# Row-wise top-10 indices: input tiles at 512-byte boundaries, batch decode spread over tiles, short last batches

## The chip, the cores and the metric

The kernel runs on one core of a Trainium2 chip. The metric is the device time of one execution, in microseconds (us): the median of three runs. Everything below on time comes from those runs and from one profiled execution of the kernel before the change.

## The reference

For every row of an 8192 x 8192 float32 matrix the reference returns the column indices of the ten largest values, ordered from the largest value down.

```python
def reference(x, k):                       # x: 8192 x 8192 float32, k = 10
    indices = np.argpartition(x, -k, axis=1)[:, -k:]
    values = np.take_along_axis(x, indices, axis=1)
    sorted_idx = np.argsort(-values, axis=1)
    return np.take_along_axis(indices, sorted_idx, axis=1)
```

The input is 268.4 MB and each element is needed once; the output is 8192 x 10 int64, 0.66 MB.

## The kernel before

The 8192 rows are worked on in 64 tiles of 128 rows. A tile is loaded as 128 partitions x 8192 float32 in such a way that one row of x is spread over eight partitions: a row is cut into R = 8 pieces of W = 1024 elements, and partition p = 8a + q holds piece q of sixteen - divided into S = 8 slots - rows. So in each partition a tile has eight runs of 4096 bytes, one for each slot. `load` (L83) issues four transfers of two slots each on the SP queue (eight of one slot for the first and the last tile). Four buffers `xt` take the tiles in turn. `load(t + 3)` is issued in the loop at tile t, and SP waits there until the gather of tile t - 1 has read the buffer for the last time.

One pass over tile t goes through these functions:

- `weigh` (L133): ScalarE computes e = exp(36 x - 169.2) of half a tile at a time (bf16, two halves), and TensorE adds up, with the 0/1 matrix `group`, the weights of the eight pieces of each row: 16 matmuls of 512 columns give `s`, which has one row of x per partition and one column per position within a piece. The largest elements dominate these sums.
- `choose` (L152): VectorE finds the G = 12 best columns of `s` for each row (MAX8, MATCH_REPLACE8, FIND_INDEX8 on 1024 elements, twice); `cidb` keeps the columns of a batch of tiles, `idx` those of this tile.
- `gather` (L178): GpSimd fetches these columns of all eight pieces out of `xt` into `cand`. It is the last reader of the `xt` buffer.
- `spread` (L190): VectorE (six columns) and GpSimd (the other six) multiply `cand` by a mask; `extract` (L204): 12 TensorE products bring the 12 x 8 candidates of a row together in `g`.
- `rank` (L211): VectorE finds the ten best of the 96 candidates and their places `posb`. This is done three tiles late (LAG = 3), step by step between the steps of `choose`.

What remains is done for a batch of TB = 8 tiles at once. `decode` (L229) turns places into column numbers with seven VectorE instructions, ending with `rows`; `deliver` (L263) moves the results of each tile of the batch to the partition of their row with one matmul `fo` each (two on the engine, for the two passes of float32); `store` (L273) copies `fo` into `opack` and writes it to DRAM from the ScalarE queue. The batches are tiles 0 to 7, 8 to 15, ..., 56 to 62, and 63 alone.

The order on every engine is the order in which the loop (L291 to L324) is written; no scheduler moves anything inside it. In tile t the loop does: `choose(t)` with `rank(t - 3)` between its steps, `spread(t - 1)`, `gather(t)`, `weigh(t + 1)`, `store` of a batch delivered in an earlier tile, `extract(t - 1)`, `deliver` of a batch decoded in an earlier tile, `decode` of a batch whose last tile was just ranked, `load(t + 3)`. Behind the loop stand the last ranks, the batch of seven tiles, the spread and extract of tile 63, and its own batch of one. At the very end a count of checks (L328 to L345) decides whether an exact, slow path runs; it does not run here.

SBUF is handed out pool by pool: `consts`, `e`, `small`, `batch`, then `x`. In the built program the four `xt` buffers begin at byte 95904, 128672, 161440 and 194208 of each partition, which is 160 past a multiple of 512 each.

Of the kernel before, what the change touches and what calls it, by code (L numbers as in the profile page):

```python
# [10 lines left out]
P = 128  # L11
N = 8192
R = 8
A = P // R
S = P // A
W = N // R
BANK = 512
KMAX = 10
G = 12
TB = 8  # L20
# [3 lines left out]
FINITE = 1e37  # L24
BIG_NEG = -1e30
LAG = 3


@with_exitstack
def kernel(  # L30
# [29 lines left out]
    epool = ctx.enter_context(tc.tile_pool(name="e", bufs=3))  # L60
    small = ctx.enter_context(tc.tile_pool(name="small", bufs=2))
    bpool = ctx.enter_context(tc.tile_pool(name="batch", bufs=2))
    xpool = ctx.enter_context(tc.tile_pool(name="x", bufs=4))
    spsum = ctx.enter_context(
        tc.tile_pool(name="spsum", bufs=2, space=bass.MemoryType.PSUM)
# [7 lines left out]

    last = ntiles - 1

    starts = list(range(0, ntiles, TB)) + [last]
    sizes = [b - a for a, b in zip(starts, starts[1:] + [ntiles])]
    batch_of = {t: b for b, t0 in enumerate(starts) for t in range(t0, t0 + sizes[b])}

# [53 lines left out]
    def weigh(t):  # L133
        ss[t] = spsum.tile([P, W], fp32, tag="s", name="s")
        parts = [S // 4, S // 4, S // 4, S // 8, S // 8] if t == last else [S // 2, S // 2]
        s0 = 0
        for h, n in enumerate(parts):
            e = epool.tile([P, S // 2, W], bf16, tag="e", name="e")
            nc.scalar.activation(  # L139
                out=e[:, 0:n, :].rearrange("p s j -> p (s j)"),  # L140
                in_=xts[t][:, s0 * W:(s0 + n) * W],
                func=ACTF.Exp, bias=bias[:, 0:1], scale=BETA,
                accum_out=eall[:, 2 * t + h:2 * t + h + 1],
            )
            for i in range(n):
                for j in range(0, W, BANK):
                    nc.tensor.matmul(ss[t][:, j:j + BANK], lhsT=group[:, s0 + i, :],  # L147
                                     rhs=e[:, i, j:j + BANK],
                                     start=s0 + i == 0, stop=s0 + i == S - 1)
            s0 += n  # L150

    def choose_steps(t):  # L152
        m = ss.pop(t)
        b = batch_of[t]
        i = t - starts[b]
        if i == 0:
            batch[b] = (
                bpool.tile([P, TB, 16], u16, tag="cidb", name="cidb"),
                bpool.tile([P, TB, 16], u16, tag="posb", name="posb"),
            )  # L160
        cid = batch[b][0][:, i, :]
        w16 = wall[:, t, :]
        m2 = small.tile([P, W], fp32, tag="m2", name="m2")
        idxs[t] = small.tile([P, G], u16, tag="idx", name="idx")
        return [
            lambda: nc.vector.max(out=w16[:, 0:8], in_=m),  # L166
            lambda: nc.vector.match_replace(out=m2, in_to_replace=w16[:, 0:8], in_values=m,  # L167
                                            imm_value=-1.0),
            lambda: nc.vector.max_index(out=cid[:, 0:8], in_max=w16[:, 0:8], in_values=m),  # L169
            lambda: nc.vector.max(out=w16[:, 8:16], in_=m2),  # L170
            lambda: nc.vector.max_index(out=cid[:, 8:16], in_max=w16[:, 8:16], in_values=m2),  # L171
            lambda: nc.vector.tensor_scalar(
                out=idxs[t], in0=cid[:, 0:G], scalar1=float(W - 1), scalar2=base,
                op0=ALU.min, op1=ALU.add,
            ),
        ]
# [11 lines left out]
        del xts[t], idxs[t]  # L188

    def spread(t):  # L190
        shape = [P, G, P // 16, 16]
        masked[t] = small.tile(shape, fp32, tag="masked", name="masked")
        cand = cands.pop(t)
        half = G // 2
        shape = [P, half, P // 16, 16]
        for eng, g0 in ((nc.vector, 0), (nc.gpsimd, half)):
            eng.tensor_tensor(  # L197
                out=masked[t][:, g0:g0 + half],
                in0=cand[:, g0:g0 + half].unsqueeze(2).to_broadcast(shape),
                in1=own.rearrange("p (c s) -> p c s", s=16).unsqueeze(1).to_broadcast(shape),  # L200
                op=ALU.mult,
            )

    def extract(t):  # L204
        mk = masked.pop(t)
        gs[t] = gpsum.tile([P, G, R], fp32, tag="g", name="g")
        for c in range(G):
            nc.tensor.matmul(gs[t][:, c, :], lhsT=mk[:, c, :, :].rearrange("p a s -> p (a s)"),  # L208
                             rhs=place, start=True, stop=True)
# [16 lines left out]
                                          in_=t8b[:, KMAX - 9:KMAX - 8]),  # L226
        ]

    def decode(b):  # L229
        cidb, posb = batch.pop(b)  # L230
        n = sizes[b]
        slot = bpool.tile([P, TB, KMAX], u16, tag="slot", name="slot")[:, 0:n, :]
        low = bpool.tile([P, TB, KMAX], u16, tag="low", name="low")[:, 0:n, :]
        nc.vector.tensor_scalar(out=slot, in0=posb[:, 0:n, 0:KMAX],
                                scalar1=R.bit_length() - 1,
                                scalar2=None, op0=ALU.logical_shift_right)
        nc.vector.tensor_scalar(out=low, in0=posb[:, 0:n, 0:KMAX], scalar1=R - 1,
                                scalar2=None, op0=ALU.bitwise_and)
        shape = [P, n, KMAX, G]
        hot = bpool.tile([P, TB, KMAX, G], fp16, tag="hot", name="hot")[:, 0:n]  # L240
        pick = bpool.tile([P, TB, KMAX], fp32, tag="pick", name="pick")[:, 0:n, :]
        nc.vector.tensor_tensor(
            out=hot, in0=slot.unsqueeze(3).to_broadcast(shape),
            in1=slots.unsqueeze(1).unsqueeze(1).to_broadcast(shape), op=ALU.is_equal,
        )
        nc.vector.tensor_tensor(
            out=hot, in0=hot, in1=cidb[:, 0:n, 0:G].unsqueeze(2).to_broadcast(shape),
            op=ALU.mult,
        )
        nc.vector.reduce_sum(out=pick, in_=hot, axis=X_AX)  # L250
        val = bpool.tile([P, TB, KMAX], fp32, tag="val", name="val")[:, 0:n, :]
        nc.vector.scalar_tensor_tensor(
            out=val, in0=low, scalar=float(W), in1=pick, op0=ALU.mult, op1=ALU.add,
        )
        shape = [P, n, A, KMAX]
        picked[b] = bpool.tile([P, TB, A, KMAX], fp32, tag="rows", name="rows")
        nc.vector.tensor_tensor(  # L257
            out=picked[b][:, 0:n], in0=val.unsqueeze(2).to_broadcast(shape),
            in1=own_a.unsqueeze(1).unsqueeze(3).to_broadcast(shape), op=ALU.mult,
        )  # L260


    def deliver(b):  # L263
        n = sizes[b]
        rows = picked.pop(b)
        fo = fpsum.tile([P, A * KMAX], fp32, tag="fo", name="fo")[0:n * S, :]
        for i in range(n):
            nc.tensor.matmul(fo, lhsT=send[:, i, 0:n * S],  # L268
                             rhs=rows[:, i].rearrange("p a k -> p (a k)"),
                             start=i == 0, stop=i == n - 1)  # L270
        ready[b] = fo

    def store(b):  # L273
        n = sizes[b]
        o = opacks[b % 2][0:n * S]
        nc.vector.tensor_copy(out=o[:, :, :, 0],
                              in_=ready.pop(b).rearrange("p (a k) -> p a k", k=KMAX))
        r0 = starts[b] * S
        nc.scalar.dma_start(out=out_rows[r0:r0 + n * S, :],
                            in_=o.rearrange("p a k two -> p (a k two)"))  # L280

    def interleave(*lists):
        for group_ in zip(*[l for l in lists if l]):
# [3 lines left out]
    def run(steps):  # L287
        for step in steps:
            step()

    with tc.manual_schedule():  # L291
        weigh(0)
        for t in range(ntiles):
            second = rank_steps(t - LAG) if t >= LAG else []
            if t == last:
                run(second)
                second = []
            interleave(choose_steps(t), second)
            if t >= 1:
                spread(t - 1)  # L300
            gather(t)
            if t + 1 < ntiles:
                weigh(t + 1)
            for b in list(ready):
                store(b)
            if t >= 1:
                extract(t - 1)
            for b in list(picked):
                deliver(b)
            if t >= LAG and batch_of[t - LAG] != batch_of[t - LAG + 1]:  # L310
                decode(batch_of[t - LAG])
            if t + 3 < ntiles:
                load(t + 3)
        run(rank_steps(last - 2))
        run(rank_steps(last - 1))
        decode(batch_of[last - 1])
        deliver(batch_of[last - 1])
        store(batch_of[last - 1])
        spread(last)
        extract(last)  # L320
        run(rank_steps(last))
        decode(batch_of[last])
        deliver(batch_of[last])
        store(batch_of[last])  # L324

# [72 lines left out]
```

## Time and profile before

| | us |
|---|---|
| median of 3 runs (lowest, highest) | 713.9 (712.68, 715.07) |
| the profiled execution | 710.63 |
| its span, first to last instruction | 708.9 |

The profiled execution is 3.3 us under the median and 2.05 us under the lowest of the three runs; 1.7 us of it lie around the span.

| engine | busy us | share of the span |
|---|---|---|
| TensorE matmul | 558.8 | 79% |
| VectorE | 559.1 | 79% |
| ScalarE | 488.9 | 69% |
| GpSimd | 180.3 | 25% |
| DMA, queue of the x loads | | 95.1% of 16 engines |

Busy time is an average over the whole span. In the profile's rows PE is the matmul side of TensorE and PEld its weight loads, DVE is VectorE, ACT ScalarE, POOL GpSimd, SP the engine that issues the x loads; a q behind an engine's name is its sequencer or queue. A DMA share over 1 means that one packet's record overlaps the next one's.

### The profile page before, as it was taken

How to read it: one execution, taken by the hardware profiler on the slowest of the kernel's cores; microseconds unless marked ns; L12 is line 12 of the kernel's file. 1: busy time of each engine (PE TensorE's matmuls, PEld its weight loads, DVE VectorE, ACT ScalarE, POOL GpSimd, SP SyncE). 2: the span in 40 equal slices, each digit the busy share in tenths (PEclk: the TensorE clock that was granted, in tenths of full speed). 3: DMA queues.
4: the chain of work that ended last, by engine and by line, in shares of the span. 5: the costliest groups of instructions: out<-in, count | busy, mean ns of one | idle time of the engine just before them, and what ended most of it. 6: DMA issues, size and time to landing. Idle time of an engine off the chain costs nothing.

```text
span 708.9 us, 7965 instructions
## 1 busy us (share of the span) xinstructions
PE 558.8 (79%) x2690; PEld 348.3 (49%) x2690; DVE 559.1 (79%) x1313; ACT 488.9 (69%) x264; POOL 180.3 (25%) x135
## 2 busy tenths in 40 slices
PE   1678988697798978788888887869877887888844
PEld 0245665464454655455556644536543653555533
DVE  1568777987879878896788887798868976888973
ACT  4777776767777677776777777677777777776800
POOL 0121322321331332233132223213322322313330
PEclk9667777987666868887777877688888786667955
DMA  8999999999999999999999999999999999999400
GB/s 350 410 408 410 408 410 408 410 409 410 409 409 409 409 409 409 410 409 409 409 409 409 408 410 409 409 409 409 410 409 409 406 408 409 410 409 386 160 1 5
DMA packets 70592, 269.69 MB, mean 380 GB/s; under 512 B 4374, under 2 KB 5014, under 8 KB 70550
## 3 DMA queue, kind: packets, MB, share of 16 engines
q1 hardware_dynamic: 69760, 268.45, 95.1%
q10 hardware_dynamic: 790, 0.73, 0.4%
q8 instruction: 21, 0.34, 0.2%
q14 instruction: 21, 0.17, 0.1%
HBM read 268.51 MB, written 0.66 MB: 380 GB/s over the span
## 4 chain that ended last, share of the span: by engine, by line
DMA 52%; DVE 22%; PE 11%; SPq 5%; ACT 4%; issue 3%; POOL 2%; ACTq 0%
DMA xt<-in_x_dram 50%; PE s L147 6%; SPq L89 5%; ACT e L139 4%; PE g L208 4%; DVE wall L166 3%; DVE m L167 3%; DVE cidb L171 2%; DVE cidb L169 2%; DMA out_dram<-opack 2%; DVE wall L170 2%; POOL cand L180 2%; DVE masked L197 2%; DVE rows L257 1%; PE fo L268 1%
## 5 line engine op out<-in xcount | busy, mean ns | idle before, releaser
L139 ACT ACTIVATE e<-xt,bias 128x4096 bf16<-128x4096 f32 (+2 forms) x131 | 475.5, 3630 | 173.5 <-DMA xt<-in_x_dram 161.0
L147 PE MATMUL s<-e,group 128*128 128x512 bf16 x1024 | 340.3, 495 | 125.6 <-ACT e L139 125.4
L147 PEld LDWEIGHTS <-group 128*128 128x128 bf16 x1024 | 124.1, 124 | 314.3 <-issue 258.0
L208 PEld LDWEIGHTS g<-cpack,masked 128*128 128x128 f32 x1536 | 208.9, 216 | 29.1 <-issue 13.9
L208 PE MATMUL g<-cpack,masked 128*128 128x8 f32 x1536 | 201.9, 270 | 11.7 <-DVE masked L197 11.6
L180 POOL INDIRECT_COPY cand<-xt,idx 128x192 f32 x64 | 64.0, 1001 | 500.9 <-DMA xt<-in_x_dram 181.8
L166 DVE MAX8 wall<-s 128x8 f32<-128x1024 f32 x64 | 78.8, 1231 | 128.9 <-PE s L147 128.9
L197 POOL TENSOR_TENSOR masked<-cand,cpack 128x768 f32<-128x768 f32 x64 | 115.4, 1802 | 5.3
L169 DVE FIND_INDEX8 cidb<-wall,s 128x8 uint16<-128x1024 f32 x64 | 78.2, 1222 | 0.0
L171 DVE FIND_INDEX8 cidb<-wall,m 128x8 uint16<-128x1024 f32 x64 | 77.9, 1217 | 0.0
L167 DVE MATCH_REPLACE8 m<-wall,s 128x1024 f32<-128x1024 f32 x64 | 77.6, 1213 | 0.0
L170 DVE MAX8 wall<-m 128x8 f32<-128x1024 f32 x64 | 77.2, 1207 | 0.0
L197 DVE TENSOR_TENSOR masked<-cand,cpack 128x768 f32<-128x768 f32 x64 | 60.6, 947 | 0.0
L268 PE MATMUL fo<-rows,send 128*64 128x160 f32 (+2 forms) x128 | 31.9, 432 | 9.5 <-DVE rows L257 9.5
L268 PEld LDWEIGHTS fo<-rows,send 128*64 128x64 f32 (+2 forms) x128 | 25.0, 203 | 13.2 <-DVE rows L257 6.2
L139 ACT ACTIVATION_READ_ACCUMULATOR e<-xt,bias 128x1 f32 x131 | 24.4, 187 | 0.0
L329 ACT ACTIVATE e<-tall,bias 128x64 f32<-128x64 f32 x1 | 0.3, 348 | 32.2 <-DVE tall L225 32.2
L219 DVE MAX8 t8a<-g 128x8 f32<-128x96 f32 x64 | 15.8, 248 | 8.1 <-PE g L208 8.1
L222 DVE FIND_INDEX8 posb<-t8a,g 128x8 uint16<-128x96 f32 x64 | 16.3, 255 | 0.0
L224 DVE FIND_INDEX8 posb<-t8b,g 128x8 uint16<-128x96 f32 x64 | 16.1, 251 | 0.0
L220 DVE MATCH_REPLACE8 g<-t8a,g 128x96 f32<-128x96 f32 x64 | 15.8, 247 | 0.0
L223 DVE MAX8 t8b<-g 128x8 f32<-128x96 f32 x64 | 15.5, 242 | 0.0
(36 smaller groups left out, 102.7 us busy)
## 6 DMA issues: line engine op xcount, KB each, us to landing
xt<-in_x_dram SPq DMA_DIRECT2D x248, 1024.0 KB, 17.1
xt<-in_x_dram SPq DMA_DIRECT2D x16, 512.0 KB, 7.4
out_dram<-opack ACTq DMA_DIRECT2D x7, 80.0 KB, 5.4
out_dram<-opack ACTq DMA_DIRECT2D x1, 70.0 KB
cpack<-topk_cpack ACTq DMA_DIRECT2D x1, 68.5 KB
out_dram<-opack ACTq DMA_DIRECT2D x1, 10.0 KB
```

The costliest lines, as they stand in the source:

```text
L89: nc.sync.dma_start(out=dst[:, s:s + n, :], in_=src[:, s:s + n, :])
L139: nc.scalar.activation(out=e[:, 0:n, :].rearrange("p s j -> p (s j)"), in_=xts[t][:, s0 * W:(s0 + n) * W], func=ACTF.Exp, bias=bias[:, 0:1 ...
L147: nc.tensor.matmul(ss[t][:, j:j + BANK], lhsT=group[:, s0 + i, :], rhs=e[:, i, j:j + BANK], start=s0 + i == 0, stop=s0 + i == S - 1)
L166: lambda: nc.vector.max(out=w16[:, 0:8], in_=m),
L167: lambda: nc.vector.match_replace(out=m2, in_to_replace=w16[:, 0:8], in_values=m, imm_value=-1.0),
L169: lambda: nc.vector.max_index(out=cid[:, 0:8], in_max=w16[:, 0:8], in_values=m),
L170: lambda: nc.vector.max(out=w16[:, 8:16], in_=m2),
L171: lambda: nc.vector.max_index(out=cid[:, 8:16], in_max=w16[:, 8:16], in_values=m2),
L180: nc.gpsimd.add_instruction(mybir.InstIndirectCopy(name=nc.get_next_instruction_name(), ins=[nc.gpsimd.lower_ap(xts[t]), nc.gpsimd.lower_a ...
L197: eng.tensor_tensor(out=masked[t][:, g0:g0 + half], in0=cand[:, g0:g0 + half].unsqueeze(2).to_broadcast(shape), in1=own.rearrange("p (c s) ...
L208: nc.tensor.matmul(gs[t][:, c, :], lhsT=mk[:, c, :, :].rearrange("p a s -> p (a s)"), rhs=place, start=True, stop=True)
L268: nc.tensor.matmul(fo, lhsT=send[:, i, 0:n * S], rhs=rows[:, i].rearrange("p a k -> p (a k)"), start=i == 0, stop=i == n - 1)
```

## The change

Three things change.

1. A tile `pad` of 88 float32 and a pool `chosen` stand ahead of the pool `x`. `cidb` and `posb` move into `chosen`, which has three buffers instead of two. In the built program `xt` now begins at byte 96768, 129536, 162304 and 195072: multiples of 512. Sizes, steps and the order of the loads stay as they were.
2. `decode`, `deliver` and `store` become one list of steps, `finish_steps`: seven VectorE steps, one matmul step per tile of the batch, a copy and the store. After a batch's last rank the list is put aside, and each of the following tiles runs three steps of it, between `extract` and `load`. For a batch of eight that is 17 steps: six tiles.
3. The batches at the end are tiles 56 to 60 (five), 61 and 62 (two) and 63 (one), instead of seven and one. Behind the loop come: what is left of the batch of 48 to 55; ranks of tiles 61 and 62; spread and extract of tile 63; the batch of five; the batch of two; the rank of tile 63; its batch of one.

```diff
+PAD = 88
...
+    pad = ctx.enter_context(tc.tile_pool(name="pad", bufs=1)).tile([P, PAD], fp32, name="pad")
+    nc.vector.memset(pad[:, 0:1], 0.0)
+    cpool = ctx.enter_context(tc.tile_pool(name="chosen", bufs=3))
     xpool = ctx.enter_context(tc.tile_pool(name="x", bufs=4))
...
-    starts = list(range(0, ntiles, TB)) + [last]
+    starts = list(range(0, ntiles, TB)) + [last - 2, last]
...
-                bpool.tile([P, TB, 16], u16, tag="cidb", name="cidb"),
-                bpool.tile([P, TB, 16], u16, tag="posb", name="posb"),
+                cpool.tile([P, TB, 16], u16, tag="cidb", name="cidb"),
+                cpool.tile([P, TB, 16], u16, tag="posb", name="posb"),
...
+    def finish_steps(b):
...
+        def move(i):
             nc.tensor.matmul(fo, lhsT=send[:, i, 0:n * S],
                              rhs=rows[:, i].rearrange("p a k -> p (a k)"),
                              start=i == 0, stop=i == n - 1)
...
+        return [
+            lambda: nc.vector.tensor_scalar(
+                out=slot, in0=posb[:, 0:n, 0:KMAX], scalar1=R.bit_length() - 1,
+                scalar2=None, op0=ALU.logical_shift_right),
...
+            lambda: nc.vector.tensor_tensor(
+                out=rows, in0=val.unsqueeze(2).to_broadcast(rshape),
+                in1=own_a.unsqueeze(1).unsqueeze(3).to_broadcast(rshape), op=ALU.mult),
+        ] + [lambda i=i: move(i) for i in range(n)] + [
+            lambda: nc.vector.tensor_copy(
+                out=o[:, :, :, 0], in_=fo.rearrange("p (a k) -> p a k", k=KMAX)),
+            lambda: nc.scalar.dma_start(out=out_rows[r0:r0 + n * S, :],
+                                        in_=o.rearrange("p a k two -> p (a k two)")),
+        ]
...
         weigh(0)
+        later = []
         for t in range(ntiles):
-            second = rank_steps(t - LAG) if t >= LAG else []
-            if t == last:
-                run(second)
-                second = []
+            second = rank_steps(t - LAG) if t >= LAG and t != last else []
             interleave(choose_steps(t), second)
...
-            for b in list(ready):
-                store(b)
             if t >= 1:
                 extract(t - 1)
-            for b in list(picked):
-                deliver(b)
-            if t >= LAG and batch_of[t - LAG] != batch_of[t - LAG + 1]:
-                decode(batch_of[t - LAG])
+            if t == last - 1:
+                run(rank_steps(last - 3))
+            for step in later[:3]:
+                step()
+            later = later[3:]
+            done = t - LAG
+            if t < last and done >= 0 and batch_of[done] != batch_of[done + 1]:
+                later += finish_steps(batch_of[done])
             if t + 3 < ntiles:
                 load(t + 3)
+        run(later)
+        later = finish_steps(batch_of[last - 3])
         run(rank_steps(last - 2))
         run(rank_steps(last - 1))
-        decode(batch_of[last - 1])
-        deliver(batch_of[last - 1])
-        store(batch_of[last - 1])
         spread(last)
         extract(last)
+        run(later)
+        run(finish_steps(batch_of[last - 1]))
         run(rank_steps(last))
-        decode(batch_of[last])
-        deliver(batch_of[last])
-        store(batch_of[last])
+        run(finish_steps(batch_of[last]))
```

VectorE at tiles 58 and 59, where the batch of tiles 48 to 55 has just been ranked. Before, the first row is the last one of tile 58's `spread`, and the last row begins `choose(59)`:

```order
L197 TENSOR_TENSOR masked<-cand,cpack 128x768
L234 TENSOR_SCALAR slot<-posb 128x80
L237 TENSOR_SCALAR low<-posb 128x80
L242 TENSOR_TENSOR hot<-slot,slots 128x960
L246 TENSOR_TENSOR hot<-hot,cidb 128x960
L250 TENSOR_REDUCE pick<-hot 128x80
L252 SCALAR_TENSOR_TENSOR val<-low,pick 128x80
L257 TENSOR_TENSOR rows<-val,cpack 128x1280
L166 MAX wall<-s 128x8
```

With the change, from the end of tile 59 to the beginning of tile 60:

```order
L201 TENSOR_TENSOR masked<-cand,cpack 128x768
L255 TENSOR_SCALAR slot<-posb 128x80
L258 TENSOR_SCALAR low<-posb 128x80
L261 TENSOR_TENSOR hot<-slot,slots 128x960
L171 MAX wall<-s 128x8
```

The first three of the seven instructions stand one tile later than before; the next three follow at the end of tile 60, and `rows` at the end of tile 61.

VectorE behind `choose(63)`, the last one (`idx` is its last step, the `masked` row is `spread(62)`). Before:

```order
L172 TENSOR_SCALAR idx<-cidb,cpack 128x12
L197 TENSOR_TENSOR masked<-cand,cpack 128x768
L219 MAX t8a<-g 128x8
L220 MATCH_REPLACE g_4181<-t8a,g 128x96
L222 MAX_INDEX posb<-t8a,g 128x8
L223 MAX t8b<-g_4181 128x8
```

With the change:

```order
L177 TENSOR_SCALAR idx<-cidb,cpack 128x12
L201 TENSOR_TENSOR masked<-cand,cpack 128x768
L274 CAST opack_139<-fo 64x160
L223 MAX t8a<-g 128x8
L224 MATCH_REPLACE g_4198<-t8a,g 128x96
L226 MAX_INDEX posb<-t8a,g 128x8
```

The copy of the results of tiles 48 to 55 now stands ahead of `rank(61)`; before it stood at the end of tile 60.

TensorE at the end, before (L208 is `extract`, the first row those of tiles 62 - its first 12 are tile 61's - and L268 the matmuls `fo`):

```order
L208 MATMUL g<-cpack,masked 128x8 x24
L268 MATMUL fo<-rows,send 56x160 x7
L208 MATMUL g<-cpack,masked 128x8 x12
L268 MATMUL fo<-rows,send 8x160
L341 MATMUL gps<-ones,ngood_4268 1x1
```

With the change:

```order
L212 MATMUL g<-cpack,masked 128x8 x12
L250 MATMUL fo<-rows,send 64x160 x3
L212 MATMUL g<-cpack,masked 128x8 x12
L250 MATMUL fo<-rows,send 64x160 x3
L212 MATMUL g<-cpack,masked 128x8 x12
L250 MATMUL fo<-rows,send 40x160 x5
L250 MATMUL fo<-rows,send 16x160 x2
L250 MATMUL fo<-rows,send 8x160
L338 MATMUL gps<-ones,ngood_4294 1x1
```

The `extract` of tile 63 (the last L212 row) now stands ahead of the matmuls of the batch that ends with it, and six matmul steps of the batch of tiles 48 to 55 stand between the last extracts.

More of the change, by code (lines that the diff above doesn't have):

```diff
@@ L190, in spread @@
     def spread(t):
-        shape = [P, G, P // 16, 16]
-        masked[t] = small.tile(shape, fp32, tag="masked", name="masked")
+        masked[t] = small.tile([P, G, P // 16, 16], fp32, tag="masked", name="masked")
         cand = cands.pop(t)
@@ L227, in rank_steps @@
         ]
-    def decode(b):
+    def finish_steps(b):
         cidb, posb = batch.pop(b)
         n = sizes[b]
+        r0 = starts[b] * S
         slot = bpool.tile([P, TB, KMAX], u16, tag="slot", name="slot")[:, 0:n, :]
         low = bpool.tile([P, TB, KMAX], u16, tag="low", name="low")[:, 0:n, :]
[L234 to L239, printed above, removed]
         hot = bpool.tile([P, TB, KMAX, G], fp16, tag="hot", name="hot")[:, 0:n]
         pick = bpool.tile([P, TB, KMAX], fp32, tag="pick", name="pick")[:, 0:n, :]
[L242 to L250, printed above, removed]
-        val = bpool.tile([P, TB, KMAX], fp32, tag="val", name="val")[:, 0:n, :]
[L252 to L265, printed above, removed]
+        val = bpool.tile([P, TB, KMAX], fp32, tag="val", name="val")[:, 0:n, :]
+        rows = bpool.tile([P, TB, A, KMAX], fp32, tag="rows", name="rows")[:, 0:n]
         fo = fpsum.tile([P, A * KMAX], fp32, tag="fo", name="fo")[0:n * S, :]
-        for i in range(n):
+        o = opacks[b % 2][0:n * S]
+        hshape = [P, n, KMAX, G]
+        rshape = [P, n, A, KMAX]
+        def move(i):
             nc.tensor.matmul(fo, lhsT=send[:, i, 0:n * S],
@@ L270, in deliver @@
                              start=i == 0, stop=i == n - 1)
[L271 to L280, printed above, removed]
+        return [
+            lambda: nc.vector.tensor_scalar(
+                out=slot, in0=posb[:, 0:n, 0:KMAX], scalar1=R.bit_length() - 1,
+                scalar2=None, op0=ALU.logical_shift_right),
+            lambda: nc.vector.tensor_scalar(
+                out=low, in0=posb[:, 0:n, 0:KMAX], scalar1=R - 1,
+                scalar2=None, op0=ALU.bitwise_and),
+            lambda: nc.vector.tensor_tensor(
+                out=hot, in0=slot.unsqueeze(3).to_broadcast(hshape),
+                in1=slots.unsqueeze(1).unsqueeze(1).to_broadcast(hshape), op=ALU.is_equal),
+            lambda: nc.vector.tensor_tensor(
+                out=hot, in0=hot, in1=cidb[:, 0:n, 0:G].unsqueeze(2).to_broadcast(hshape),
+                op=ALU.mult),
+            lambda: nc.vector.reduce_sum(out=pick, in_=hot, axis=X_AX),
+            lambda: nc.vector.scalar_tensor_tensor(
+                out=val, in0=low, scalar=float(W), in1=pick, op0=ALU.mult, op1=ALU.add),
+            lambda: nc.vector.tensor_tensor(
+                out=rows, in0=val.unsqueeze(2).to_broadcast(rshape),
[6 more added lines that the diff above has]
+        ]
     def interleave(*lists):
```

## The prediction, on record before the changed kernel ran

> **What bounds the kernel now.** I read the slices of the span first, since a kernel with every engine below 80% must be waiting for something, then the stretches, the waits, and the timeline of the end. The DMA share and what it moved, in 40 slices of 17.7 us:
>
> ```profile
> DMA  8999999999999999999999999999999999999400
> GB/s 350 410 408 410 408 410 408 410 409 410 409 409 409 409 409 409 410 409 409 409 409 409 408 410 409 409 409 409 410 409 409 406 408 409 410 409 386 160 1 5
> ```
>
> The loads run without a pause from the first slice to the 37th, at 408 to 410 GB/s, and then some 45 us follow without them. So the time is the stream of loads and a tail. Stretches (us from the span's start; length; busy time of each engine; granted clock; DMA share; GB/s):
>
> ```profile
> core 0: us, PE busy (x) PEld busy (x) DVE busy (x) ACT busy (x) POOL busy (x), PEclk, DMA share, GB/s
> 4.00:8.00 4.00, 0.00 (x0) 0.10 (x1) 1.41 (x17) 0.00 (x0) 0.00 (x0) 1.00 1.03 422
> 8.00:12.00 4.00, 0.00 (x0) 0.00 (x0) 0.00 (x0) 3.34 (x2) 0.00 (x0) 1.00 1.03 414
> 12.00:20.00 8.00, 5.09 (x16) 1.89 (x16) 0.52 (x1) 6.62 (x5) 0.00 (x0) 1.00 1.03 410
> ...
> 300.00:600.00 300.00, 245.00 (x1215) 154.00 (x1215) 248.50 (x574) 219.77 (x116) 81.23 (x58) 0.78 1.03 409
> 600.00:638.00 38.00, 33.45 (x157) 19.21 (x157) 31.19 (x71) 27.48 (x17) 8.44 (x6) 0.68 1.03 409
> 638.00:641.00 3.00, 1.67 (x4) 0.46 (x3) 3.00 (x8) 3.00 (x2) 2.70 (x2) 0.50 0.89 325
> 641.00:646.00 5.00, 4.33 (x15) 1.75 (x14) 5.00 (x13) 3.71 (x3) 0.00 (x0) 0.65 1.00 400
> ```
>
> Two things matter here. The DMA share is full (1.03) from 4 us on: the loads never wait for a buffer, but for one dip at 638. And the same 4096-byte packets go at 422 GB/s in the first microseconds and at 409 ever after. 16 engines x 4096 bytes give one packet per engine in 155 ns at 422 and in 160 ns at 409.
>
> Who waits for the loads, and what the SP queue waits for:
>
> ```profile
> ACT e L139 <- DMA xt<-in_x_dram: 161.0, 118, 2.4
> ```
>
> ```profile
> SPq L89 <- POOL cand L180: 291.0, 60, 7.6
> ...
> SPq L89 <- DMA out_dram<-opack: 13.6, 7, 7.1
> ```
>
> ```profile
> xt<-in_x_dram SPq DMA_DIRECT2D x248, 1024.0 KB, 17.1
> ```
>
> ScalarE waits for data 118 times, at nearly each of its pieces. SP waits 291 us for the gathers to free a buffer, which costs nothing: a transfer of 1 MB lands 17.1 us (median) after it is issued, where 2.6 us would move it at 409 GB/s, so some 14 us of work lie ahead of it in the queue.
>
> The tail, from the timeline (start us, us, engine, line, what; idle time before it):
>
> ```profile
> 658.57 3.71 ACT L139 ACTIVATE e<-xt,bias 128x4096 bf16<-128x4096 f32 x1 [0.75 <-DMA xt<-in_x_dram]
> 662.28 1.99 ACT L139 ACTIVATE e<-xt,bias 128x2048 bf16<-128x2048 f32 x1
> 664.35 1.23 DVE L166 MAX8 wall<-s 128x8 f32<-128x1024 f32 x1 [0.70 <-PE s L147]
> 673.63 1.22 DVE L166 MAX8 wall<-s 128x8 f32<-128x1024 f32 x1
> 680.01 0.95 DVE L197 TENSOR_TENSOR masked<-cand,cpack 128x768 f32<-128x768 f32 x1
> 681.11 5.26 PE L208 MATMUL g<-cpack,masked 128*128 128x8 f32 x24 [5.85 <-DVE masked L197]
> 685.42 1.79 POOL L197 TENSOR_TENSOR masked<-cand,cpack 128x768 f32<-128x768 f32 x1
> 686.41 0.27 DVE L219 MAX8 t8a<-g 128x8 f32<-128x96 f32 x1 [4.09 <-PE g L208]
> 687.83 0.19 DVE L234 TENSOR_SCALAR slot<-posb 128x70 uint16<-128x70 uint16 x1
> 692.46 3.71 PE L268 MATMUL fo<-rows,send 128*56 128x160 f32 x14 [6.09 <-DVE rows L257]
> 696.20 0.32 DVE L276 CAST opack<-fo 56x160 uint32<-56x160 f32 x1 [3.80 <-PE fo L268]
> 696.44 0.94 DVE L197 TENSOR_TENSOR masked<-cand,cpack 128x768 f32<-128x768 f32 x1
> 697.53 3.78 PE L208 MATMUL g<-cpack,masked 128*128 128x8 f32 x24 [1.36 <-DVE masked L197]
> 701.34 0.27 DVE L219 MAX8 t8a<-g 128x8 f32<-128x96 f32 x1 [3.96 <-PE g L208]
> 702.77 0.18 DVE L234 TENSOR_SCALAR slot<-posb 128x10 uint16<-128x10 uint16 x1
> 704.75 0.69 PE L268 MATMUL fo<-rows,send 128*8 128x160 f32 x2 [3.45 <-DVE rows L257]
> 705.48 0.31 DVE L276 CAST opack<-fo 8x160 uint32<-8x160 f32 x1 [0.88 <-PE fo L268]
> ```
>
> The second half of tile 62 reaches ScalarE at 658.57; from there everything follows on VectorE: `choose(62)` at 664.35, `choose(63)` at 673.63, `spread(62)` at 680.01. Tile 63's own data is no wait (662.28 has none). From 680 on VectorE and TensorE take turns until 705.8.
>
> **The boundary of xt.** Nothing is added on the path: one VectorE memset ahead of the first load, while VectorE is idle (1.41 us busy in the 4 us at 4). What it may move is the 409 GB/s. At 4 to 12 us TensorE and GpSimd do nothing and VectorE next to nothing, yet the rate falls from 422 to 414 and 410, and it stays at 409 whatever the engines do later. So the DMA engines can do 422, and something behind them takes only 409 once a backlog stands: either the side that reads x, which the change leaves alone, or the side that writes into SBUF, where each 4096-byte run began 160 bytes past a 512-byte boundary and now begins on one. No row holds a load to another offset, so the trace can't tell the two apart. Bounds: nothing, if it is the reading side; and the pace of the 422 row, the highest any row shows, if it is the writing side. From 12 to 638 us that is 626 x (1 - 409/422) = 19.3 us, with the last two tiles nearly 20. A loss by the boundary itself I exclude: a run that begins on a boundary touches no more blocks, of any size that divides 512 bytes, than a shifted one. I take 19.5: a limit that sets in only after a few microseconds of faster packets, in a stretch where nothing else uses SBUF, looks like a queue in front of the writes that has filled; reads that were too slow would more likely have been so at once. That is a reading, not a proof, and gets six chances in ten.
>
> The Trainium skill, "DMA: Bandwidth & Descriptors", section "How a descriptor splits into AXI transactions", says that a descriptor is moved in transactions of 256 bytes that must start at 256-byte boundaries, with the surplus of the first one still paid for. By its count a 4096-byte run that starts 160 bytes past such a boundary takes 133 beats in place of 128, which by estimate would take 645 x 5/133 = 24 us off the 645 us of stream, and the time would be some 5 us lower than my sum. The page tells this of fetched bytes; that the writing side pays as well, no row here shows.
>
> At 422 GB/s a tile comes every 9.9 us instead of 10.3 us. ScalarE needs 2 x 3.9 us for it, VectorE 248.5/300 x 10.3 = 8.5 us with the decodes (7.9 without, since one of about 5 us falls on eight tiles), and the 14 us in the queue ahead of an issue become 0.4 us less, so the engines follow.
>
> **The decode in pieces.** Before, the seven instructions ran in one go, and their place in the chain of waits is this:
>
> ```profile
> 632.48 1.11 DVE hot L242
> ...
> 637.26 1.14 DVE wall L166
> ```
>
> They hold `choose(59)`, and with it the gather that frees the buffer, for nearly 5 us. The only dip this makes is the one at 638: 3 x 84/409 + 5 x 9/409 = 0.7 us. In pieces, the dearest three steps are the second multiplication, the sum and `val`, of which two have these rows:
>
> ```profile
> L250 DVE TENSOR_REDUCE pick<-hot 128x80 f32<-128x960 f16 x7 | 8.1, 1153 | 0.2
> L246 DVE TENSOR_TENSOR hot<-hot,cidb 128x960 f16<-128x960 f16 x7 | 4.6, 658 | 0.2
> ```
>
> With `val` that is about 2 us, within the 2.4 us that VectorE has left in a tile of 10.3 us, and just filling a tile of 9.9. So the dip goes: -0.7 us. The work is the same; with faster loads the one lump would have made longer dips, so its cover matters more then. The stores move from four tiles earlier; SP waited 13.6 us for them in all, 7.1 us once, at the last pieces of tile 63, which nobody waited for. The last full batch is now stored behind the loop, so that wait goes and gains nothing.
>
> **The end.** The steps up to `spread(62)` (680.96) stay. Then `run(later)` puts the copy of the batch of 48 to 55 first on VectorE, and it waits for three matmul steps behind `extract(62)` on TensorE: 686.37 + 6 x 0.265 (3.71 us for 14) = 688.0. Queued behind it are both ranks and `spread(63)`, for which the tail waits. Copy 0.3, ranks of 61 and 62 1.42 each (686.41 to 687.83), `spread(63)` 0.95: done at 692.1, not 697.4. `extract(63)` at 3.8 ends at 695.9; the decode of five tiles (seven took 4.63, from 687.83 to 692.46, one 1.98; so some 3.7) is hidden behind it. Ten matmuls 2.65, copy 0.35: 698.9. Decode of two 2.2, four matmuls 1.1, copy 0.4: 702.6. `rank(63)` 1.43, decode of one 1.98, its matmuls 0.73: the last copy begins at 706.7, not 705.48: +1.2 us. What goes behind `extract(63)` is paid back by the copy that comes first and by a third batch. The clock of TensorE gives the bounds:
>
> ```profile
> 672.40:675.30 2.90, 2.85 (x24) 2.75 (x24) 2.83 (x13) 0.00 (x0) 0.00 (x0) 0.99 0.00 0
> 681.00:686.40 5.40, 5.26 (x24) 5.20 (x24) 1.25 (x9) 0.00 (x0) 1.99 (x2) 0.50 0.01 3
> ```
>
> The same 24 matmuls take 2.85 us at a clock of 0.99 and 5.26 at 0.50. `extract(63)` at 5.26 makes it +2.7; at 2.85, with the 14 matmuls behind it at half their time, -1.6.
>
> **The sum.** -19.5 - 0.7 + 1.2 = -19.0 us. On the profiled execution's own time of 710.6 this gives 691.6; its runs lie 3.3 us higher in the median, so 713.9 - 19.0 = 695.
>
> **The rivals.** (a) The reading side sets the 409. Then the boundary does nothing: -0.7 + 1.2 = +0.5, about 714.4. For it: the rate is the same to 1 in 400 from 20 us to 638. Against it: the 422 at the start. (b) The loads get faster only in part, or the gain is lost to late gathers: SP's issues still hang on GpSimd's gather, and in one tile of eight the dearest pieces load VectorE with 9.9 us, all that a tile at 422 has. Half the gain: about 704. For it: the dip at 638 shows that a late gather does reach the loads; against: that took 5 us of delay at once, and here there is none to begin with. (c) Slower: the boundary does nothing, and the copy that is now first behind `spread(62)` holds both ranks while TensorE stays at its low clock, as it was at 681. From an `extract(63)` of 5 us on, this decides: +2.7 us without the dip's gain, 716.6.
>
> **Chances.** The forecast 0.52, (b) 0.12, (a) 0.26, (c) 0.10. What lies within 0.3% (2.1 us) can't be told from no change with runs like these. So faster 0.64, same 0.26, slower 0.10. The range goes from 691, past which only a rate above 422 leads, up to 715.5, to hold rival (a); the forecast's own is 691 to 699.
>
> **What would show it.** Right: the slices at 420 or more from the second on, the loads' last slice one earlier, the wait of ScalarE for data still its largest. The stretch after 638 has no dip. The copy `opack` behind `spread(62)` waits 7 us for `fo`. Wrong: slices at 409 again, with a tail 1 us longer, or slices that fall below 100% share: then gathers bound the loads.

## The result and the profile after

The changed kernel takes 697.5 us (median of four runs, 696.5 to 699.2) against 714.45 us for the kernel before (712.7 to 715.1): a ratio of 0.977 with a 95% interval of 0.974 to 0.980, 16.9 us. The median of before is now of four runs, one more than ahead of the prediction. The forecast was 695, the range 691 to 715.5. The profiled execution took 696.5, with a span of 694.7 us; the span of before was 708.9.

The slices of the span, kernel after:

```profile
DMA  8999999999999999999999999999999999999100
GB/s 356 421 419 421 419 421 419 421 419 421 419 419 421 420 420 419 421 419 421 420 420 420 419 421 420 420 420 421 419 420 421 420 420 420 420 420 408 53 6 5
```

From the second slice to the 36th every one moves 419 to 421 GB/s, where before it was 408 to 410 but for one of 406. The stretches, with columns as before:

```profile
4.00:8.00 4.00, 0.00 (x0) 0.10 (x1) 1.42 (x17) 0.00 (x0) 0.00 (x0) 1.00 1.03 420
8.00:12.00 4.00, 0.00 (x0) 0.00 (x0) 0.00 (x0) 3.52 (x2) 0.00 (x0) 1.00 1.03 422
12.00:20.00 8.00, 6.15 (x16) 2.07 (x16) 0.08 (x1) 6.86 (x5) 0.00 (x0) 1.00 1.02 420
...
300.00:600.00 300.00, 251.06 (x1233) 160.72 (x1256) 255.70 (x593) 223.80 (x117) 82.50 (x59) 0.77 1.03 420
...
620.00:640.00 20.00, 17.76 (x73) 11.20 (x73) 17.11 (x39) 15.14 (x8) 4.69 (x4) 0.59 1.03 418
```

The pace of the first microseconds, which before sank to 409 by 20 us, now lasts to the end, and the dip that stood at 638 us is gone: from 620 to 640 us, up to the arrival of tile 62, the rate is 418. ScalarE still waits mostly for data, a little less:

```profile
ACT e L144 <- DMA xt<-in_x_dram: 146.3, 117, 2.2
```

The end on the timeline:

```profile
640.73 3.71 ACT L144 ACTIVATE e<-xt,bias 128x4096 bf16<-128x4096 f32 x1 [1.09 <-DMA xt<-in_x_dram]
645.89 1.48 DVE L270 TENSOR_TENSOR rows<-val,cpack 128x1280 f32<-128x1280 f32 x1
647.29 1.22 DVE L171 MAX8 wall<-s 128x8 f32<-128x1024 f32 x1
656.57 1.22 DVE L171 MAX8 wall<-s 128x8 f32<-128x1024 f32 x1
662.96 0.95 DVE L201 TENSOR_TENSOR masked<-cand,cpack 128x768 f32<-128x768 f32 x1
664.05 5.26 PE L212 MATMUL g<-cpack,masked 128*128 128x8 f32 x24 [4.89 <-DVE masked L201]
671.14 0.32 DVE L274 CAST opack<-fo 64x160 uint32<-64x160 f32 x1 [7.24 <-PE fo L250]
674.07 0.95 DVE L201 TENSOR_TENSOR masked<-cand,cpack 128x768 f32<-128x768 f32 x1
675.16 5.26 PE L212 MATMUL g<-cpack,masked 128*128 128x8 f32 x24 [4.06 <-DVE slot L255]
680.36 2.89 PE L250 MATMUL fo<-rows,send 128*40 128x160 f32 x10
683.28 0.32 DVE L274 CAST opack<-fo 40x160 uint32<-40x160 f32 x1 [4.76 <-PE fo L250]
687.02 0.31 DVE L274 CAST opack<-fo 16x160 uint32<-16x160 f32 x1 [1.41 <-PE fo L250]
691.38 0.31 DVE L274 CAST opack<-fo 8x160 uint32<-8x160 f32 x1 [0.88 <-PE fo L250]
```

The second half of tile 62 reaches ScalarE at 640.73, 17.8 us earlier than before (658.57). `choose(62)` begins at 647.29, 17.1 us earlier: it now stands behind `rows` of the batch of 48 to 55, which costs 0.8 us. From `spread(62)` to the last copy it takes 691.38 - 662.96 = 28.4 us, where before it was 705.48 - 680.01 = 25.5. So in the two profiled executions the stream gives 17.8 us, and the end takes 3.7 back: 14.1 us, which is the difference of the spans to within 0.1. The medians differ by 2.8 us more: the profiled execution of before was 3.8 us under its median (710.6 and 714.45), that of the changed kernel 1.0 under its own.

### The profile page after: what moved, and what is told of

Same layout as the page of the kernel before. It is cut to its first block, busy times and chain, and to the rows that moved or that the text cites. A ratio compares the mean times of both kernels' runs of the same rounds, so it can differ in the third digit from the quotient of the medians.

```text
span 694.7 us, 7933 instructions
## 1 busy us (share of the span) xinstructions
PE 551.4 (79%) x2645; PEld 348.0 (50%) x2690; DVE 559.2 (80%) x1322; ACT 488.7 (70%) x264; POOL 181.2 (26%) x135
## 4 chain that ended last, share of the span: by engine, by line
DMA 54%; PE 15%; DVE 13%; SPq 6%; ACT 6%; issue 4%; POOL 2%; ACTq 0%
DMA xt<-in_x_dram 52%; PE s L152 9%; SPq L94 6%; ACT e L144 6%; PE g L212 5%; DVE wall L171 2%; DMA out_dram<-opack 2%; POOL cand L185 2%; DVE m L172 2%; PE fo L250 1%; DVE cidb L176 1%; DVE cidb L174 1%; DVE wall L175 1%; DVE masked L201 1%; DVE g L224 0%
## 5 line engine op out<-in xcount | busy, mean ns | idle before, releaser
L152 PE MATMUL s<-e,group 128*128 128x512 bf16 x979 | 330.7, 493 | 122.8 <-ACT e L144 118.9
L152 PEld LDWEIGHTS <-group 128*128 128x128 bf16 x1024 | 121.8, 122 | 306.4 <-issue 249.4
L212 PEld LDWEIGHTS g<-cpack,masked 128*128 128x128 f32 x1536 | 215.4, 222 | 27.1 <-issue 15.8
L212 PE MATMUL g<-cpack,masked 128*128 128x8 f32 x1536 | 207.7, 274 | 11.1 <-DVE masked L201 6.6
L250 PE MATMUL fo<-rows,send 128*64 128x160 f32 (+3 forms) x128 | 29.2, 375 | 6.2 <-DVE rows L270 6.2
L250 PEld LDWEIGHTS fo<-rows,send 128*64 128x64 f32 (+3 forms) x128 | 18.3, 160 | 9.3 <-issue 7.3
L226 DVE FIND_INDEX8 posb<-t8a,g 128x8 uint16<-128x96 f32 x64 | 16.4, 256 | 0.0
```

The lines of the kernel that those rows point to most:

```text
L250: nc.tensor.matmul(fo, lhsT=send[:, i, 0:n * S], rhs=rows[:, i].rearrange("p a k -> p (a k)"), start=i == 0, stop=i == n - 1)
```

## The experiments

Two theories were to be told apart. Theory 1: the boundary of `xt` sets the rate of the loads, and the rest of the change costs a little. Theory 2: the loads were held by the decode in one lump, and the boundary does nothing. After that came the questions which boundary it is, on which side of a transfer it counts, and what the new end costs.

All of these kernels leave out GpSimd's gather. In its place stand one copy of `idx` and eight plain copies out of `xt`, so that the buffer is still given back only after `idx` is known. The candidates are then not those of the reference, and the comparison of the last check is turned round so that the exact path stays unused:

```diff
-        nc.gpsimd.add_instruction(mybir.InstIndirectCopy(...))
+        nc.gpsimd.tensor_copy(out=cands[t][:, :, 0], in_=idxs[t])
+        for i in range(8):
+            nc.gpsimd.tensor_copy(out=cands[t].rearrange("p g s -> p (g s)"),
+                                  in_=xts[t][:, i * 192:(i + 1) * 192])
...
-    out=..., in0=e10, scalar=SLACK, in1=wall[:, :, G], op0=ALU.mult, op1=ALU.is_gt,
+    out=..., in0=e10, scalar=-SLACK, in1=wall[:, :, G], op0=ALU.mult, op1=ALU.is_lt,
```

### The two controls

> Control: the kernel before, with GpSimd's gather replaced by one copy of idx and eight plain copies of 192 columns out of xt, so that the buffer is still given back only after idx is known; the candidates are therefore not those of the reference, and the last check's comparison is turned so that the exact path stays unused. Everything else as before. Both theories expect the stream of loads to be untouched: 409 GB/s in the middle of the span, about 714 us (711 to 717).

> Control: the changed kernel with the same stand-in for the gather (same part of the computation left out). Both theories expect what the change showed with the real gather: 420 GB/s in the middle, about 697.5 us, ratio 0.977.

The control of before took 712.65 us against 712.6 for the kernel before on the same chip: ratio 1.001 (1.000 to 1.003). The control of the changed kernel took 698.3 us, ratio 0.981 (0.978 to 0.984), faster, though the interval reaches to both sides of 2%. The loads go at the rates of the kernels that they stand for, although the stand-in keeps GpSimd about twice as long. First the control of before, then that of the changed kernel:

```profile
300.00:600.00 300.00, 251.12 (x1215) 159.21 (x1215) 250.44 (x576) 219.68 (x116) 165.68 (x287) 0.76 1.03 409
```

```profile
300.00:600.00 300.00, 257.34 (x1261) 159.36 (x1260) 257.43 (x595) 224.23 (x119) 175.92 (x300) 0.77 1.03 420
```

Their ends, from `spread(62)` to the last copy (VectorE on the timeline), first before, then changed:

```profile
680.04 0.95 DVE L194 TENSOR_TENSOR masked<-cand,cpack 128x768 f32<-128x768 f32 x1
...
705.52 0.31 DVE L273 CAST opack<-fo 8x160 uint32<-8x160 f32 x1 [0.88 <-PE fo L265]
```

```profile
665.48 0.95 DVE L198 TENSOR_TENSOR masked<-cand,cpack 128x768 f32<-128x768 f32 x1
673.67 0.32 DVE L271 CAST opack<-fo 64x160 uint32<-64x160 f32 x1 [7.24 <-PE fo L247]
...
693.91 0.31 DVE L271 CAST opack<-fo 8x160 uint32<-8x160 f32 x1 [0.87 <-PE fo L247]
```

25.5 us and 28.4 us, as with the gather itself. But `spread(62)` begins 2.5 us later in this control than in the changed kernel (665.48 and 662.96). From 647.0 to 652.2 us its TensorE had a granted clock of 0.50, and the 24 matmuls of `extract(61)` took 5.12 us there; in the changed kernel it was 1.00 from 646.3 to 649.0 and the same matmuls took 2.74. `choose(63)` follows 2.5 us later. So two traces can differ by that much ahead of the end, and the ends are compared here from `spread(62)` on.

### The boundary alone, and everything but the boundary

```diff
 # s_before_aligned: on the control of before
+    pad = ctx.enter_context(tc.tile_pool(name="pad", bufs=1)).tile([P, 88], fp32, name="pad")
+    nc.vector.memset(pad[:, 0:1], 0.0)
     xpool = ctx.enter_context(tc.tile_pool(name="x", bufs=4))
 # s_after_160: on the control of the changed kernel
-PAD = 88
+PAD = 128
```

> The control of before, with nothing but a pad that puts xt on 512-byte boundaries; decode in one lump, batches of seven and one at the end (same part left out). Theory 1 (the boundary sets the rate of the loads): 420 GB/s and nearly all of the gain, 695 to 698 us; the lumps show as dips of about 1 us each, at most. Theory 2 (the lump of decode was what held the loads back, the boundary does nothing): 409 GB/s, 714 us.

> The control of the changed kernel with the pad chosen so that xt is 160 bytes past a 512-byte boundary again, as before; decode spread and short last batches stay (same part left out). Theory 1: 409 GB/s again, 714 to 717 us, the tail some 3 us longer than before's and the dip at 638 gone. Theory 2: 420 GB/s, 698 us.

The boundary alone: 695.3 us, ratio 0.9775 (0.9752 to 0.9798), 17.2 us off. Everything but the boundary: 714.5 us, ratio 1.003 (1.001 to 1.005), 1.9 us on top of the kernel before. The stretch from 300 to 600 us, boundary alone and then all but the boundary:

```profile
300.00:600.00 300.00, 256.12 (x1257) 161.26 (x1257) 255.78 (x593) 223.76 (x118) 171.25 (x300) 0.77 1.02 419
```

```profile
300.00:600.00 300.00, 250.40 (x1214) 152.38 (x1213) 252.48 (x582) 219.91 (x116) 170.17 (x290) 0.75 1.03 409
```

The rate goes with the boundary, whichever decode stands beside it. Theory 2 falls. The 419 where the changed kernel has 420 is the lump, which makes dips in the loads. Two of them, boundary alone:

```profile
545.00:560.00 15.00, 11.80 (x57) 9.26 (x57) 11.39 (x29) 9.15 (x5) 9.71 (x20) 0.77 1.02 412
570.00:577.00 7.00, 5.55 (x34) 3.23 (x33) 7.00 (x17) 4.90 (x3) 4.76 (x8) 1.00 1.02 404
```

15 x 8/420 and 7 x 16/420 us: 0.3 us each. In the same two stretches the kernels with the decode in pieces show none: 419 and 420 GB/s in the control of the changed kernel, 410 and 408 at 160 bytes. Such dips do not need the faster loads. The kernel before has one at 396 GB/s from 565 to 570 us (0.2 us) besides that at 638, and the two kernels with the lump at 64 and 128 bytes of the next section fall to 396 and 395 from 555 to 570.

The boundary alone is 3.0 us faster than the control of the whole change (693.6 to 696.9 against 697.5 to 700.3, on the same chip): what the spreading spares the loads is less than what the new end costs, which from `spread(62)` on is 28.4 us against 25.5.

### Which boundary

```diff
+    pad = ... .tile([P, 104], ...)   # xt  64 past a 512-byte boundary
+    pad = ... .tile([P, 120], ...)   # xt 128 past one
+    pad = ... .tile([P,  24], ...)   # xt 256 past one
```

> The control of before (gather replaced by plain copies, so the candidates are not the reference's) with a pad that puts xt 64 bytes past a 512-byte boundary. If each byte ahead of the boundary costs in proportion (160 bytes cost 409 against 420 GB/s), 64 bytes cost 4 GB/s: about 416. If any start off the boundary costs the same: 409. If only a start off a 64-byte boundary costs: 420.

> The same with xt 128 bytes past a 512-byte boundary (same part left out). In proportion: about 411 GB/s. Any start off the boundary the same: 409. Only the 64-byte or 128-byte boundary: 420.

> The same with xt 256 bytes past a 512-byte boundary (same part left out). If the boundary that counts is one of 256 bytes, as a page's rule of 256-byte transactions would have it: 420 GB/s, about 695 us. If it is one of 512 bytes: 409, about 713 us.

One execution each: 714.4, 711.8 and 698.3 us beside one of the kernel before of 711.7. Single times say little here; the rates, each an average over 200 us of steady loads, decide. Stretches at 64, at 128 and at 256 bytes past the boundary:

```profile
4.00:8.00 4.00, 0.00 (x0) 0.10 (x1) 1.42 (x17) 0.00 (x0) 0.00 (x0) 1.00 1.02 418
...
12.00:20.00 8.00, 5.59 (x16) 1.93 (x16) 0.43 (x1) 6.62 (x5) 0.00 (x0) 1.00 1.03 410
100.00:300.00 200.00, 162.44 (x783) 102.03 (x797) 164.38 (x381) 146.16 (x79) 110.69 (x193) 0.78 1.03 409
```

```profile
4.00:8.00 4.00, 0.00 (x0) 0.10 (x1) 1.42 (x17) 0.00 (x0) 0.00 (x0) 1.00 1.04 424
...
12.00:20.00 8.00, 5.46 (x16) 1.91 (x16) 0.34 (x1) 6.63 (x5) 0.00 (x0) 1.00 1.03 410
100.00:300.00 200.00, 162.00 (x783) 100.65 (x797) 164.39 (x381) 146.35 (x79) 110.50 (x193) 0.78 1.03 409
```

```profile
100.00:300.00 200.00, 166.16 (x812) 103.80 (x825) 170.75 (x390) 151.06 (x79) 114.63 (x196) 0.77 1.03 420
```

A start at 64, 128 or 160 bytes costs the same 11 GB/s, a start at 0 or 256 nothing. So it is a boundary of 256 bytes, not of 512, and at these five offsets it is missed or met: 64 bytes past it are no cheaper than 160. The pad and its memset stand in the slow kernels too, so neither is what helps. Both kernels off the boundary start quicker (418 and 424 GB/s) and have sunk to 410 by the stretch from 12 to 20 us, as before.

The Trainium skill, "DMA: Bandwidth & Descriptors", section "How a descriptor splits into AXI transactions", has the 256 bytes: transactions of 256 bytes from 256-byte boundaries. The runs agree with that. They do not agree with a price by the bytes ahead of the start, of which a start 64 bytes past the boundary should have paid less: the rows at 64 and 160 are the same 409. What fits them is the count of blocks that a 4096-byte run touches, 17 in place of 16, whatever part of the first is used; that is a reading of five offsets, and the runs do not show the mechanism itself. In size the count alone does not fit: 17 for 16 would be 6%, and 409 against 420 is 2.6%. It would fit if writes on the boundary could go at some 409 x 17/16 = 435 GB/s (an estimate) and something else held the loads at 420 there; no run here shows that.

### Which side of the transfer

```diff
-        src = x[t * P:(t + 1) * P, :].rearrange("(s a) (q j) -> (a q) s j", a=A, q=R)
+        o = t * P * N + (40 if t < ntiles - 1 else 0)
+        src = x.rearrange("r c -> (r c)")[o:o + P * N].rearrange(
+            "(s a q j) -> (a q) s j", a=A, q=R, j=W)
```

> The control of before with xt on 512-byte boundaries, but the loads of tiles 0 to 62 read x from 160 bytes further on, so that now every read starts 160 bytes past a boundary and every write on one (the values are shifted, and the gather is left out as in the control). If a start off a boundary costs the reading side as it costs the writing side: 409 GB/s, 713 us. If only the writing side pays: 420, 695 us.

One execution: 693.35 us, and

```profile
100.00:300.00 200.00, 165.12 (x820) 105.89 (x833) 172.58 (x396) 151.24 (x79) 116.60 (x200) 0.80 1.03 420
300.00:600.00 300.00, 251.93 (x1236) 162.31 (x1259) 255.80 (x593) 224.19 (x120) 172.38 (x300) 0.78 1.03 420
```

Reads that begin 160 bytes further on cost this kernel nothing; writes into SBUF that begin 160 bytes past a boundary cost 11 GB/s. Where x itself begins in memory is not on record, but 160 is no multiple of 256, so of this kernel and the one with the boundary alone at least one reads off a 256-byte boundary, and they run at 420 and 419. The section of the Trainium skill named above tells of the surplus for bytes that are fetched; here it is the writing side that pays.

### What the end costs, and a better one

The first kernel changes one number in the changed kernel's control, the second the order of the end behind the boundary alone. The third stands on the changed kernel's control and has both, with batches of seven and one again:

```diff
 # s_after_early_copy
-            for step in later[:3]:
+            now = 6 if t == last - 1 else 3
+            for step in later[:now]:
                 step()
-            later = later[3:]
+            later = later[now:]
 # s_lump_tail (batches of seven and one); s_spread_tail has the same order with finish_steps
         run(rank_steps(last - 2))
         run(rank_steps(last - 1))
+        spread(last)
+        extract(last)
         decode(batch_of[last - 1])
         deliver(batch_of[last - 1])
-        store(batch_of[last - 1])
-        spread(last)
-        extract(last)
         run(rank_steps(last))
         decode(batch_of[last])
+        store(batch_of[last - 1])
         deliver(batch_of[last])
         store(batch_of[last])
```

> The control of the changed kernel (gather replaced by plain copies, 698.3 us), with six steps instead of three at tile 62, so that the last three matmuls of the batch of tiles 48 to 55 stand ahead of the last extract(62) and the copy behind spread(62) waits for nothing. Theory: that copy, with both ranks and spread(63) queued behind it on VectorE, costs about 4 us: from spread(62) to the last copy 24.4 us instead of 28.4, 694.3 us. Rival: the last three short batches with a copy each are what costs, and the gain is under 1 us.

> The control of before on 512-byte boundaries (695.3 us; gather replaced by plain copies), with decode in lumps and batches of seven and one as before; only the end is in another order: spread(63) and extract(63) ahead of the decode of seven, and rank(63) with its decode ahead of the copy of seven, so that VectorE and TensorE work side by side. Expected from rows: from spread(62) to the last copy 18.4 us instead of 25.5, 688 to 689 us. If the lumps of decode cost the loads nothing, this is as fast as the next kernel.

> The control of the changed kernel (boundary, decode spread; gather replaced by plain copies) with batches of seven and one at the end, six steps at tile 62, and the same order of the end as the kernel with lumps beside it. Expected: 18.4 us from spread(62) to the last copy, 688 us. Against the kernel with lumps: if spreading the decode keeps the loads from the dips that the lumps make with faster loads (1 to 2 us), it is that much faster; if the pieces hold choose(62) as the changed kernel's did (0.8 us), the two agree.

Measured: 694.7 us, ratio 0.972 (0.970 to 0.975); 687.6 us, ratio 0.963 (0.961 to 0.965); 687.0 us, ratio 0.962 (0.960 to 0.964). VectorE from `spread(62)` to the last copy, in this order:

```profile
665.44 0.95 DVE L198 TENSOR_TENSOR masked<-cand,cpack 128x768 f32<-128x768 f32 x1
666.31 0.31 DVE L271 CAST opack<-fo 64x160 uint32<-64x160 f32 x1
...
671.84 0.27 DVE L220 MAX8 t8a<-g 128x8 f32<-128x96 f32 x1 [3.88 <-PE g L209]
...
690.51 0.31 DVE L271 CAST opack<-fo 8x160 uint32<-8x160 f32 x1 [0.88 <-PE fo L247]
```

```profile
663.97 0.95 DVE L196 TENSOR_TENSOR masked<-cand,cpack 128x768 f32<-128x768 f32 x1
...
682.37 0.31 DVE L275 CAST opack<-fo 8x160 uint32<-8x160 f32 x1 [0.53 <-PE fo L267]
```

```profile
662.93 0.95 DVE L198 TENSOR_TENSOR masked<-cand,cpack 128x768 f32<-128x768 f32 x1
...
680.98 0.32 DVE L273 CAST opack<-fo 56x160 uint32<-56x160 f32 x1 [0.64 <-PE fo L249]
681.83 0.31 DVE L273 CAST opack<-fo 8x160 uint32<-8x160 f32 x1 [0.53 <-PE fo L249]
```

25.1 us, 18.4 and 18.9, where the control of the changed kernel took 28.4. In the first, the copy that waited 7.24 us now runs at once, `rank(61)` runs beside `extract(62)`, and the wait of 3.88 us is only that for `rank(62)`: 3.4 us won, of 4 expected. That copy, held up by three matmuls behind `extract(62)`, accounts for the 2.9 us by which the changed end was longer. The other order, in which VectorE ranks and decodes tile 63 while TensorE still sends the batch of seven, wins 7.1 us over the end of before. Lumps or pieces make no difference that these runs can tell: 687.6 and 687.0, with intervals that overlap. In the two traces the pieces bring `spread(62)` 1.0 us earlier and lose 0.5 us behind it. Both beat the changed kernel's control, by 11 us in the medians; these were taken on two chips, and by the ratios to the kernel before on the same chip it is 13. With the gather itself this order was not run.

## Why the prediction was right

**What bounds the kernel**: right. ScalarE waited for the loads, the loads never for a buffer, and what made the loads faster made the kernel faster.

**The boundary**: right in kind. Of the reason given for it, the writing side is shown: reads off the boundary cost nothing, writes off it 11 GB/s, and on it the early pace lasts. That the limit sets in because a backlog fills a queue fits the rates off the boundary, which are at 410 from 12 us on, but no run shows the queue. One premise was misread: from 8 to 12 us, where "nothing else uses SBUF", ScalarE was busy 3.34 of 4 us. The changed kernel clears it: there ScalarE is busy 3.52 of the same 4 us at 422 GB/s. The size was somewhat too large. The forecast took the 422 of the first stretch, worth 19.5 us; the kernel settles at 420: 626 x (1 - 409/420) = 16.4 us to 638, and with the last two tiles and the dip the data came 17.8 us earlier, where the sum had 20.2. The first stretch was a measure of four microseconds. What the trace of before couldn't give, other offsets, has now been measured: each of the five gives 409 or 420. The estimate of 24 us from the beats of the Trainium skill was too large by more.

**The decode in pieces**: -0.7 us for the dip was right: with the pieces at 160 bytes the loads go at 410 GB/s from 638 to 641 us, where the control of before has 356. It was not the only dip, as the prediction has it; the 32nd slice of before, at 406, holds the beginning of the small one at 565 us. That the pieces would fit into the tile without a price was wrong in one place: `rows` holds `choose(62)` by 0.8 us. And that the lump would make longer dips with faster loads is not seen: with the boundary alone the two measured are 0.3 us each.

**The end**: the direction, the place and the mechanism were right: the copy behind `spread(62)` waits (7.24 us, 7 forecast), and the step that follows, `spread(63)`, ends 5.3 us sooner. 17.05 us earlier by the shift of `spread(62)`, the forecast's times become: copy 671.0 (measured 671.14), `spread(63)` done 675.1 (675.02), last copy 689.7 (691.38). The 1.7 us missing are `extract(63)`: 5.26 us, the bound at the low clock, where 3.8 was taken, and ten matmuls at 2.89 where 2.65 was. The 3.8 came from the row of before, where `extract(63)` stood 1.4 us behind 14 matmuls at a granted clock of 0.71; in its new place, behind an idle time of 4.06 us, the clock was 0.50. So +2.9 us instead of +1.2; with the 0.8 above, the end cost 3.7.

**The sum**: both misses go the same way, 2.4 us of loads and 2.5 us of end. Between the two profiled executions, on whose rows the sum was built, the gain is 14.1 us and not 19.0, 696.5 us where it gave 691.6. The medians differ by 16.9. The 2.8 us between the two measures lie in which executions were profiled, and no trace shows where in the kernel they fall. And a range up to 715.5 holds rival (a) too: the time alone would have decided little, the rate of the loads did.

**The rivals**: (a) and (c) fall with the rate of 420. The mechanism of (c), the copy with the ranks behind it at a low clock, is real; the copy's wait cost 3.4 us, but did not decide. (b) did not come to pass: at 420 GB/s nothing lagged but for the 0.8 us.

## What to carry to other kernels

When loads run at a constant rate whatever the engines do, compare it with the rate of the first microseconds. Here a gap between the two, 422 against 409 GB/s, came from the address at which the transfers write, so that address is worth an early look. For a kernel bound by such loads, start the destination of every run on a 256-byte boundary: it takes one pad and was worth 17 us here. And when work is cut up and run later, see where its last piece lands: here it was a copy in front of the ranks at the end, and it took back a fifth of the gain.

## What the runs showed of the hardware that was not expected

That a start off a boundary is paid in full or not at all: 409 GB/s at 64, 128 and 160 bytes past a 512-byte boundary, and 420 at 0 and 256 past one. That reading side and writing side differ: reads moved on by 160 bytes, 420. And the clock of TensorE at the end: in the changed kernel the same 24 matmuls took 5.26 us in both of the last extracts, at a granted clock of 0.50, though six other matmuls had been put between them.
